# Seven products in place of eight for one more pair of feed-forward groups, with two of four weight-block sums made by adding DMAs

## The chip, the cores and the metric

The kernel runs on one core of a Trainium2 chip. The metric is device time in microseconds (us). The engines are named as in the profile: PE (TensorE, matmul), DVE (VectorE), ACT (ScalarE), POOL (GpSimd) and SP (SyncE, which in this kernel issues all loads).

## The reference

Two stacks of two layers each are applied to one sequence of 256 tokens of width 1024, in float32. Each layer is feed-forward, mixer, feed-forward, with norms between; so there are eight feed-forwards and four mixers. The change concerns the feed-forwards, which all have a hidden width of 2816:

```python
D_MODEL = 1024
SEQ = 256
DEPTH = 2
D_FF = 2816
...
def swiglu(x, w13, w2):
    a, b = jnp.split(x @ w13, 2, axis=-1)
    return (jax.nn.silu(a) * b) @ w2
...
    for l in range(DEPTH):
        x = layer_norm(ALPHA * x + 0.5 * swiglu(x, ffn1_w13[l], ffn1_w2[l]), ln_g[l, 0], ln_b[l, 0])
        m = mixer(x, w_in[l], lower_bounds[l], hg_norm_g[l], sg_ln_g[l], sg_ln_b[l], sg_ws[l],
                  sg_bs[l], w_branch_a[l], w_branch_b[l], w_out[l])
        x = layer_norm(ALPHA * x + m, ln_g[l, 1], ln_b[l, 1])
        x = layer_norm(ALPHA * x + 0.5 * swiglu(x, ffn2_w13[l], ffn2_w2[l]), ln_g[l, 2], ln_b[l, 2])
```

## The kernel before

The 256 tokens are two tiles of 128, i = 0 and 1. All weights stream from HBM as blocks of 128 x 1024 float32 (512 KB), each used once; the host lays them out in the order of use (`_ffn_units`, `_stream`). One such block is a unit. SP loads it (`fetch`) into a stage tile `stg`, or, if it belongs to a pair (below), into a tile `raw` of the pool `whp`. Then `split` makes two parts of it: ACT rounds it to `wh` (line 268), DVE subtracts and gets `wl` (line 274). A product of float32 accuracy is three matmuls with 512 moving columns: x-high with `wh`, x-high with `wl`, x-low with `wh`. Units that are not of a pair are split in two halves of 512 columns (two ACT and two DVE instructions); in mixer 2 POOL subtracts the second half of every third unit between 8 and 28. Units of a pair are split whole.

A feed-forward has 11 groups of 256 hidden columns (4 units each, gate and up part side by side) and 22 units of the output matrix (rows, "r"). The first two groups (`OWN`) are done by each token tile for itself. Then `joint` runs a hand-written list, `FFN`, for both tiles at once: ("g", n) is group n done plainly; ("r", k) is output row block k; ("s", n, ks...) is a pair, `pair`: groups n and n + 1 together, as a 2 x 2 by 2 x 2 block product after Strassen and Winograd. Its four weight blocks are called 11, 12, 21, 22 (half of the contraction, gate or up); seven products p1, p2, q5, p3, p6, p7, q4 take the place of eight, each with two units and 12 matmuls (line 547). Four of the seven need sums of weight blocks. DVE makes these in place in the `raw` tiles (`operand`): for q5 and p6 at line 245, for p7 at 249, for q4 at 253, each twice per pair. The ks are output rows that `on` runs for both tiles in the gaps after the products listed in `GAPS`. After some products ACT copies the PSUM bank to a tile `kp`/`kq` (501), DVE adds to it (504), ACT takes silu, DVE multiplies (511), and two steps later PE transposes the result (286; its high and low parts are then made at 294 and 295). The last six output rows (`LAST`) run tile by tile.

How far `split` runs ahead of the matmuls is set by `lead`: PAIR units within reach of a pair, otherwise LEAD plus up to MORE. Loads run STAGES = 4 units ahead of `split`. PE, DVE and ACT orders come out of a scheduler; SP and POOL run in program order. POOL does the power in each norm (410, 619), some mixer work, and, in four of the feed-forwards, products of gain rows (570, 631, 633).

Of the kernel before, what the change touches and what calls it, by code (L numbers as in the profile page):

```python
# [11 lines left out]
F32 = mybir.dt.float32  # L12
# [3 lines left out]
ALU = mybir.AluOpType  # L16
# [3 lines left out]
P = 128  # L20
# [16 lines left out]
RAMP = 3  # L37
STEP = 1
TAIL = 2
PAIR = 5  # L40
LAGS = dict(ffn=9, mixer1=6, mixer2=6)
STAGES = 4
SLOTS = 31
# [10 lines left out]


OWN = 2
FFN = (("g", 8), ("s", 2, 0, 1, 2, 3), ("g", 9), ("s", 4, 16, 17, 4, 5), ("g", 10), ("s", 6, 6, 7, 18, 19),
       ("r", 8), ("r", 9), ("r", 20), ("r", 21))
LAST = (10, 11, 12, 13, 14, 15)


PRODUCTS = ("p1", "p2", "q5", "p3", "p6", "p7", "q4")
LOADS = dict(p1="11", p2="21", q5="12", p3="22")
BLOCKS = ("11", "21", "12", "22")
GAPS = ("p1", "q5", "p6", "p7")


PRM_BS, PRM_LB, PRM_CW, PRM_CB, PRM_N = 0, 8, 16, 96, 112
# [6 lines left out]
def hs(h):  # L75
    return slice(h * P, (h + 1) * P)


class Core:
# [125 lines left out]
    def lead(self):  # L205
# [3 lines left out]
        left = dict(ffn=len(_ffn_units()), mixer1=56, mixer2=36)[kind] - n  # L209
        if self.product(min(self.pos[0] + PAIR, self.nunit - 1)):  # L210
            return PAIR
        return LEAD + (MORE if n < FIRST else max(0, MORE - left // RAMP))
# [11 lines left out]
    def fetch(self, v):  # L224
        while self.next_dma <= min(v, self.nunit - 1):
            made = self.made[self.next_dma]
            if not self.product(self.next_dma):
                t = self.stages[self.next_dma] = self.stg.tile([P, 1024], F32, tag="stg", name=self.nm("stg"))
                for c in (slice(0, 512), slice(512, 1024)) if self.next_dma == 0 else (slice(0, 1024),):
                    self.nc.sync.dma_start(t[:, c], self.a["ws"][made][:, c])  # L230
            elif made[0] in LOADS:
                t = self.raw[made[:2]] = self.whp.tile([P, 1024], F32, tag="w", name=self.nm("raw"))
                self.nc.sync.dma_start(t, self.block(LOADS[made[0]], *made[1:]))
            self.next_dma += 1

# [3 lines left out]
    def operand(self, p, u, base):  # L239


        raw, add = self.raw, self.nc.vector.tensor_add
        if p in ("q5", "p6"):
            t = raw["p1", u]
            add(t, t, raw["q5" if p == "q5" else "p3", u])  # L245
            return t
        if p == "p7":
            t = raw.pop(("p3", u))
            add(t, t, raw.pop(("q5", u)))  # L249
            return t  # L250
        if p == "q4":
            t = raw.pop(("p1", u))
            add(t, t, raw.pop(("p2", u)))  # L253
            return t
        return raw[p, u]

    def split(self, u):
        while self.next_split <= min(u, self.nunit - 1):
            v = self.next_split
            self.fetch(v)  # L260
            made = self.made[v]
            product = self.product(v)
            w = self.operand(*made) if product else self.stages.pop(v)
            hi = self.whp.tile([P, 1024], F32R, tag="w", name=self.nm("wh"))
            lo = self.whp.tile([P, 1024], F32R, tag="w", name=self.nm("wl"))
            halves = [slice(0, 512), slice(512, 1024)]
            for h, c in enumerate([slice(0, 1024)] if product else halves):
                r = self.nc.scalar.activation(hi[:, c], w[:, c], AF.Copy)  # L268
                if v < 3:
                    self.pin(r)  # L270
                if h and self.pool_share(*self.phase[v]):
                    self.nc.gpsimd.tensor_tensor(lo[:, c], w[:, c], hi[:, c], op=ALU.subtract)
                else:
                    self.nc.vector.tensor_sub(lo[:, c], w[:, c], hi[:, c])  # L274
            self.units[v] = [hi[:, c] for c in halves], [lo[:, c] for c in halves]
            self.next_split += 1
            self.fetch(v + STAGES)

    def pool_share(self, kind, n):
# [177 lines left out]
    def joint(self, J, rs):  # L457

        for what, n, *ks in FFN:
            if what == "s":  # L460
# [28 lines left out]
    def pair(self, J, g, ks):  # L489

        nc = self.nc
        first = dict(p1="p1", p2="p2", q5="q5", p3="q5", p6="p1", p7="p1", q4="p1")
        bank, kept, sg = {}, {}, {}
        rows = dict(zip(GAPS[len(GAPS) - len(ks):], ks))

        def keep(p):
            t = kept[p] = self.slot(name="k" + p)  # L500
            nc.scalar.activation(t, bank[p], AF.Copy)  # L501

        def add(t, other):
            nc.vector.tensor_add(t, t, other)  # L504

        def silu(out, src, i):
            rs = J["rs", i]
            nc.scalar.activation(out, src, AF.Silu, scale=1.0 if rs is None else rs)

        def hidden(i, t, sg):  # L510
            nc.vector.scalar_tensor_tensor(t, t, -0.5 if J["rs", i] is None else -1.0, sg,
                                           op0=ALU.mult, op1=ALU.mult)

            def turn():
                hi, lo = self.to_T(t, "hT")
                for c in range(4):
                    J["h", i, 2 * g + c] = hi[:, hs(c)], lo[:, hs(c)]

            self.later(2, turn)

        def after(p):
            if p in ("p1", "q5", "p6", "p7"):
                keep(p)
            if p == "p2":
                t = sg[0] = kept.pop("p1")
                add(t, bank[p])
                silu(t, t, 0)
            elif p == "p6":
                t = kept.pop("p6")
                add(t, bank["p3"])  # L530
                hidden(0, t, sg.pop(0))
            elif p == "p7":
                add(kept["p7"], kept.pop("q5"))
            elif p == "q4":
                t = self.slot(name="sg")
                silu(t, bank[p], 1)
                hidden(1, kept.pop("p7"), t)

        for p in PRODUCTS:
            bank[p] = self.bank(self.grp, "g") if first[p] == p else bank[first[p]]  # L540
            xh, xl = J["X"][p]
            for u in range(2):
                wh, wl = self.units[self.pos[1]]
                for j in range(2):
                    k = 2 * u + j
                    for q, (x, w) in enumerate(((xh, wh), (xh, wl), (xl, wh))):
                        nc.tensor.matmul(bank[p], x[:, hs(k)], w[j], start=first[p] == p and k + q == 0,  # L547
                                         stop=k == 3 and q == 2, skip_group_check=True)
                for i in range(2):
                    self.pos[i] += 1  # L550
                if u:
                    after(p)
                yield
            if p in rows:
                yield from self.on(J, rows[p])
# [1044 lines left out]
```

## Time and profile before

| what | value |
|---|---|
| median of 3 runs | 2171.57 us (2169.29 to 2174.26) |
| the profiled execution's own time | 2170.61 us |
| its span, first to last instruction | 2168.8 us |
| mean granted clock of TensorE | 0.995 |
| busy: PE, DVE, ACT, POOL | 2116.2, 1879.8, 1352.0, 291.4 us |
| HBM read | 391.63 MB |

The span is what the trace covers; the own time has 1.8 us more around it. Busy time is the time in which an engine has at least one instruction in flight, so a pipelined engine can be busy throughout and yet be slower than it could be.

### The profile page before, as it was taken

To read this page: it belongs to the slowest core of one execution; us is meant where nothing else is said; L and a number is where in the kernel's file an instruction comes from. 1 tells how busy PE (TensorE), PEld (TensorE's weight loads), DVE (VectorE), ACT (ScalarE), POOL (GpSimd) and SP (SyncE) were. 2 spreads that over 40 slices of the span, in tenths; PEclk is the share of its full clock that TensorE was granted. 3 is DMA by queue.
4 is the path that set the end of the run, shared out by engine and by line. 5 is a ranking of instruction groups with operands and counts; after the bars stand their busy time and mean duration, and the time that the engine had idled before them with its cause. 6 is when DMAs were issued, how large, how long until landed. Compare 5 with 4: busy or idle time off the path is not lost.

```text
span 2168.8 us, 28670 instructions
## 1 busy us (share of the span) xinstructions
PE 2116.2 (98%) x9968; PEld 1738.6 (80%) x9968; DVE 1879.8 (87%) x2837; ACT 1352.0 (62%) x2351; POOL 291.4 (13%) x319
## 2 busy tenths in 40 slices
PE   8999999999999999999999999999999999999998
PEld 6877888888788788888778787788778878788887
DVE  7998787899889879698989988689998998877995
ACT  6665755566566575565656665666666666576663
POOL 0000420000000033000100304610200010550000
PEclk9999999999999999999999999999999999999999
DMA  8547455455654655545555553434655546343552
GB/s 301 185 176 244 148 190 193 141 213 201 208 190 175 218 160 180 178 159 197 199 197 203 204 194 122 165 117 148 233 195 186 182 172 219 111 152 127 205 192 97
DMA packets 115296, 394.55 MB, mean 182 GB/s; under 512 B 12880, under 2 KB 15312, under 8 KB 115152
## 3 DMA queue, kind: packets, MB, share of 16 engines
q1 hardware_dynamic: 115152, 392.73, 52.5%
q8 instruction: 78, 1.28, 0.2%
q14 instruction: 66, 0.54, 0.1%
HBM read 391.63 MB, written 1.05 MB: 181 GB/s over the span
## 4 chain that ended last, share of the span: by engine, by line
PE 80%; DVE 10%; issue 3%; ACT 3%; POOL 2%; DMA 2%; SPq 0%; DVEq 0%; POOLq 0%; ACTq 0%
PE g L302 33%; PE big L302 23%; PE g L547 17%; DVE wl L274 5%; PE g L286 4%; ACT wh L268 2%; DMA stg<-in_ws_dram 2%; PE big L1262 1%; PE big L1291 1%; PE big L792 1%; DVE raw L245 1%; DVE kp L504 0%; DVE raw L249 0%; PE big L1209 0%; POOL cu L1135 0%
## 5 line engine op out<-in xcount | busy, mean ns | idle before, releaser
L274 DVE TENSOR_TENSOR wl<-stg,wh 128x512 fp32r<-128x512 f32 x1026 | 691.8, 708 | 129.6 <-ACT wh L268 123.3
L268 ACT ACTIVATE wh<-stg 128x512 fp32r<-128x512 f32 x1040 | 600.8, 623 | 200.8 <-PE g L302 83.8
L302 PE MATMUL g<-wh,xh 128*128 128x512 f32 x1184 | 483.1, 408 | 9.3 <-ACT wh L268 5.9
L302 PE MATMUL g<-wl,xh 128*128 128x512 f32 x1184 | 467.2, 395 | 0.5 <-DVE wl L274 0.5
L302 PE MATMUL g<-wh,xl 128*128 128x512 f32 x1184 | 465.3, 395 | 0.0
L268 ACT ACTIVATE wh<-raw 128x1024 fp32r<-128x1024 f32 x336 | 349.3, 1056 | 178.1 <-DVE raw L253 53.7
L274 DVE TENSOR_TENSOR wl<-raw,wh 128x1024 fp32r<-128x1024 f32 x336 | 410.2, 1236 | 25.1 <-ACT wh L268 23.1
L302 PEld LDWEIGHTS g<-wh,xh 128*128 128x128 f32 x1184 | 225.5, 190 | 58.8 <-ACT wh L268 7.3
L302 PEld LDWEIGHTS g<-wh,xl 128*128 128x128 f32 x1184 | 224.7, 190 | 50.4 <-DVE xl L311 2.0
L302 PEld LDWEIGHTS g<-wl,xh 128*128 128x128 f32 x1184 | 225.7, 191 | 43.4 <-DVE wl L274 1.8
L302 PE MATMUL big<-wh,hT 128*128 128x512 f32 x640 | 183.3, 390 | 0.0
L547 PE MATMUL g<-wh,Xh 128*128 128x512 f32 x384 | 149.7, 390 | 1.1 <-ACT kp L501 1.1
L547 PE MATMUL g<-wl,Xh 128*128 128x512 f32 x384 | 150.7, 393 | 0.0
L547 PE MATMUL g<-wh,Xl 128*128 128x512 f32 x384 | 150.2, 391 | 0.0
L302 PEld LDWEIGHTS big<-wh,hT 128*128 128x128 f32 x640 | 120.1, 188 | 25.3
L410 POOL TENSOR_TENSOR m<-m,nhalf 128x1 f32<-128x1 f32 (+1 forms) x24 | 23.1, 962 | 794.5 <-DVE m L409 794.5
L302 PE MATMUL big<-wh,hTh 128*128 128x512 f32 x384 | 124.8, 392 | 0.0
L302 PE MATMUL big<-wl,hTh 128*128 128x512 f32 x384 | 124.2, 390 | 0.0
L302 PE MATMUL big<-wh,hTl 128*128 128x512 f32 x384 | 124.0, 390 | 0.0
L245 DVE TENSOR_TENSOR raw<-raw,raw 128x1024 f32<-128x1024 f32 x96 | 120.6, 1268 | 0.5
L547 PE MATMUL g<-wh,xh 128*128 128x512 f32 x288 | 114.6, 398 | 1.4 <-ACT kp L501 1.4
L547 PE MATMUL g<-wl,xh 128*128 128x512 f32 x288 | 112.5, 391 | 0.0
(322 smaller groups left out, 3229.2 us busy)
## 6 DMA issues: line engine op xcount, KB each, us to landing
stg<-in_ws_dram SPq DMA_DIRECT2D x519, 512.0 KB, 4.4
raw<-in_ws_dram SPq DMA_DIRECT2D x192, 512.0 KB, 5.0
row<-in_norm_gain_dram SPq DMA_DIRECT2D x24, 256.0 KB, 6.8
row<-in_ln_g_dram SPq DMA_DIRECT2D x12, 256.0 KB, 4.9
row<-in_ln_b_dram SPq DMA_DIRECT2D x12, 256.0 KB, 6.3
xT<-in_xT_dram SPq DMA_DIRECT2D x4, 256.0 KB, 6.1
x<-in_x_dram SPq DMA_DIRECT2D x4, 256.0 KB, 8.7
out_dram<-x SPq DMA_DIRECT2D x4, 256.0 KB, 2.0
```

The lines of the kernel that those rows point to most:

```text
L245: add(t, t, raw["q5" if p == "q5" else "p3", u])
L268: r = self.nc.scalar.activation(hi[:, c], w[:, c], AF.Copy)
L274: self.nc.vector.tensor_sub(lo[:, c], w[:, c], hi[:, c])
L286: self.nc.tensor.transpose(tp[:, hs(j)], src[:, hs(j)], self.ident)
L302: self.nc.tensor.matmul(accs[c], a, b[c], start=start and q == 0, stop=stop and q == 2)
L410: self.nc.gpsimd.tensor_tensor(out, out, self.nhalf[:, 0:n], op=ALU.pow)
L547: nc.tensor.matmul(bank[p], x[:, hs(k)], w[j], start=first[p] == p and k + q == 0, stop=k == 3 and q == 2, skip_group_check=True)
L792: nc.tensor.matmul(ps[:, 64 * h:64 * h + 64].rearrange("p (c m) -> p c m", m=m), Z[:, hs(h)], view(Z[:, hs(h)], m)[:, :, 1, :], start=True ...
L1262: nc.tensor.matmul(ps[:, hh * S + j * P:hh * S + j * P + P], J["aq", i][r, hs(head // 2)], J["ak", j][r, hs(head // 2)], start=True, stop= ...
L1291: nc.tensor.matmul(o[:, 64 * hh:64 * hh + 64], pT[:, hs(2 * hh + j)], J["av", j][:, head * 64:head * 64 + 64], start=j == 0, stop=j == 1)
```

## The change

There are now four pairs and three plain groups per feed-forward (before: three and five). The order of the seven products is p1, q5, p3, p6, p2, p7, q4. DVE still makes the sums for q5 and p6, in the same tiles. The sums for p7 and q4 are made by DMA: as soon as p6's block has been split, POOL issues two DMAs that load a weight block from HBM a second time and add it onto the tile that lies there already (`added`): block 12 onto the tile of p3, block 21 onto that of p1. That is four such DMAs per pair, 128 in all, of 512 KB each. Units outside of pairs are split whole instead of by halves (all but the first eight of the program and those that POOL shares). PAIR goes from 5 to 6. The list of output rows in the gaps and the weights' layout follow.

```diff
-PAIR = 5
+PAIR = 6
...
-FFN = (("g", 8), ("s", 2, 0, 1, 2, 3), ("g", 9), ("s", 4, 16, 17, 4, 5), ("g", 10), ("s", 6, 6, 7, 18, 19),
-       ("r", 8), ("r", 9), ("r", 20), ("r", 21))
-LAST = (10, 11, 12, 13, 14, 15)
-
-
-PRODUCTS = ("p1", "p2", "q5", "p3", "p6", "p7", "q4")
-LOADS = dict(p1="11", p2="21", q5="12", p3="22")
-BLOCKS = ("11", "21", "12", "22")
-GAPS = ("p1", "q5", "p6", "p7")
+FFN = (("g", 10), ("s", 2, 0, 1, 2, 3), ("s", 4, 20, 21, 4, 5), ("s", 6, 6, 7, 8, 9), ("s", 8, 10, 11, 12),
+       ("r", 13))
+LAST = (14, 15, 16, 17, 18, 19)
+
+
+PRODUCTS = ("p1", "q5", "p3", "p6", "p2", "p7", "q4")
+LOADS = dict(p1="11", q5="12", p3="22", p2="21")
+BLOCKS = ("11", "12", "22", "21")
+GAPS = ("q5", "p6", "p2", "p7")
...
         if p in ("q5", "p6"):
-            t = raw["p1", u]
-            add(t, t, raw["q5" if p == "q5" else "p3", u])
+            t = raw["p1", u, base]
+            add(t, t, raw.pop(("q5", u, base)) if p == "q5" else raw["p3", u, base])
             return t
-        if p == "p7":
-            t = raw.pop(("p3", u))
-            add(t, t, raw.pop(("q5", u)))
-            return t
-        if p == "q4":
-            t = raw.pop(("p1", u))
-            add(t, t, raw.pop(("p2", u)))
-            return t
-        return raw[p, u]
+        return raw.pop((dict(p7="p3", q4="p1").get(p, p), u, base)) if p in ("p2", "p7", "q4") else raw[p, u, base]
+
+    def added(self, p, u, base):
+        if p == "p6":
+            for q, b in (("p3", "12"), ("p1", "21")):
+                self.nc.gpsimd.dma_start(self.raw[q, u, base], self.block(b, u, base), accum_op=ALU.add)
...
-            for h, c in enumerate([slice(0, 1024)] if product else halves):
+            for h, c in enumerate([slice(0, 1024)] if product or v >= 8 and not self.pool_share(*self.phase[v]) else halves):
...
             self.next_split += 1
+            if product:
+                self.added(*made)
...
-            if p == "p2":
-                t = sg[0] = kept.pop("p1")
+            if p == "p6":
+                add(kept["p6"], bank["p3"])
+            elif p == "p2":
+                t = kept.pop("p1")
                 add(t, bank[p])
                 silu(t, t, 0)
-            elif p == "p6":
-                t = kept.pop("p6")
-                add(t, bank["p3"])
-                hidden(0, t, sg.pop(0))
+                hidden(0, kept.pop("p6"), t)
```

The first place is DVE's order in the first pair of the second feed-forward. Before, from p3's second block (first row) to p7's first block (last row); L249 and L253 are the sums for p7 and q4, `stg` are gap rows:

```order
L274 TENSOR_TENSOR wl_3963<-raw_3897,wh_3962 128x1024
L249 TENSOR_TENSOR raw_3872<-raw_3872,raw_3739 128x1024
L274 TENSOR_TENSOR wl_3976<-raw_3649,wh_3975 128x1024
L249 TENSOR_TENSOR raw_3897<-raw_3897,raw_3848 128x1024
L504 TENSOR_TENSOR kp_940_3929<-kp_940_3929,g_3955 128x512
L274 TENSOR_TENSOR wl_3988<-raw_3681,wh_3987 128x1024
L274 TENSOR_TENSOR wl_4014<-stg_3953,wh_4013 128x512 x2
L253 TENSOR_TENSOR raw_3649<-raw_3649,raw_3714 128x1024
L274 TENSOR_TENSOR wl_4021<-raw_3872,wh_4020 128x1024
```

In the changed kernel the stretch of the same pair from p6's first block (`raw_3468`, the tile of p1) to p7's first block (`raw_3539`, the tile of p3) reads, with L271 for the subtraction, L245 for the sum for p6, `raw_3711` and `raw_3739` for the two blocks of p2:

```order
L271 TENSOR_TENSOR wl_3734<-raw_3468,wh_3733 128x1024
L245 TENSOR_TENSOR raw_3492<-raw_3492,raw_3559 128x1024
L441 SCALAR_TENSOR_TENSOR sg_3701<-g_3630,sg_3701 128x256
L271 TENSOR_TENSOR wl_3751<-raw_3492,wh_3750 128x1024
L441 SCALAR_TENSOR_TENSOR sg_3704<-g_3631,sg_3704 128x256
L450 TENSOR_TENSOR hT_3723<-g_3720,hT_3723 128x256
L271 TENSOR_TENSOR wl_3774<-stg_3687,wh_3773 128x1024
L271 TENSOR_TENSOR wl_3778<-raw_3711,wh_3777 128x1024
L450 TENSOR_TENSOR hT_3729<-g_3726,hT_3729 128x256
L271 TENSOR_TENSOR wl_3794<-raw_3739,wh_3793 128x1024
L271 TENSOR_TENSOR wl_3812<-stg_3756,wh_3811 128x1024
L271 TENSOR_TENSOR wl_3816<-raw_3539,wh_3815 128x1024
```

The sums for p7 and q4 have left DVE, the gap rows' pairs of half subtractions have become one, and five other blocks stand between the split of p6's first block and that of p7's first block.

The second place is POOL's queue in a feed-forward of the second stack. Before, between the powers of two norms (L410, L619) there are only the products of gain rows:

```order
L619 TENSOR_TENSOR m_10404<-m_10404,nhalf 128x1
L631 TENSOR_TENSOR xg_11244<-x_10267,row_11097 128x512
L633 TENSOR_TENSOR gg_11246<-row_11093,row_11097 128x512
L631 TENSOR_TENSOR xg_11245<-x_10271,row_11099 128x512
L633 TENSOR_TENSOR gg_11247<-row_11095,row_11099 128x512
L631 TENSOR_TENSOR xg_11358<-x_10393,row_11097 128x512
L631 TENSOR_TENSOR xg_11359<-x_10397,row_11099 128x512
L619 TENSOR_TENSOR m_11888<-m_11888,nhalf 128x1
```

In the changed kernel the same products of gain rows (L629, L631) stand behind the adding DMAs of three pairs and ahead of those of the fourth:

```order
L252 DMA raw_10636<-in_ws_dram 128x1024
L252 DMA raw_10554<-in_ws_dram 128x1024
L629 TENSOR_TENSOR xg_10752<-x_9779,row_10588 128x512
L631 TENSOR_TENSOR gg_10754<-row_10584,row_10588 128x512
L629 TENSOR_TENSOR xg_10753<-x_9783,row_10590 128x512
L631 TENSOR_TENSOR gg_10755<-row_10586,row_10590 128x512
L629 TENSOR_TENSOR xg_10839<-x_9899,row_10588 128x512
L629 TENSOR_TENSOR xg_10840<-x_9903,row_10590 128x512
L252 DMA raw_10881<-in_ws_dram 128x1024
L252 DMA raw_10816<-in_ws_dram 128x1024
...
L617 TENSOR_TENSOR m_11337<-m_11337,nhalf 128x1
```

The adding DMAs are new in this queue; each waits there, in order, for the DVE and ACT instructions that still read its tile.

## Rows read from the trace of the kernel before

**Rows 1.** The page, part 1: busy us, share of the span, instructions.

```profile
PE 2116.2 (98%) x9968; PEld 1738.6 (80%) x9968; DVE 1879.8 (87%) x2837; ACT 1352.0 (62%) x2351; POOL 291.4 (13%) x319
```

**Rows 2.** The page, part 4: chain that ended last, share of the span.

```profile
PE 80%; DVE 10%; issue 3%; ACT 3%; POOL 2%; DMA 2%; SPq 0%; DVEq 0%; POOLq 0%; ACTq 0%
```

**Rows 3.** Timeline of PE, six matmuls of a pair: start, duration, what.

```profile
1005.06 0.39 PE L547 MATMUL g<-wh,xh 128*128 128x512 f32 x1
...
1006.20 0.39 PE L547 MATMUL g<-wh,xl 128*128 128x512 f32 x1
1006.43 0.27 PE L286 MATMUL g<-con,sg 128*128 128x128 f32 x1
```

**Rows 4.** Groups of PE: count, busy us, mean ns, idle before.

```profile
L302 PE MATMUL g<-wh,xh 128*128 128x512 f32 x1184 | 483.1, 408 | 9.3 <-ACT wh L268 5.9 <-ACT xh L310 3.1 <-ACT xh L164 0.2
...
L547 PE MATMUL g<-wh,Xh 128*128 128x512 f32 x384 | 149.7, 390 | 1.1 <-ACT kp L501 1.1
```

**Rows 5.** Waits of PE: us in total, times, longest.

```profile
PE g L286 <- DVE x L593: 10.3, 10, 1.4
PE g L286 <- DVE kp L511: 7.3, 6, 1.8
...
PE g L286 <- DVE sg L445: 4.8, 7, 0.9
...
PE g L547 <- ACT kp L501: 2.5, 2, 1.4
```

**Rows 6.** Windows in one feed-forward: PE, PEld, DVE, ACT, POOL busy, clock, DMA share, GB/s.

```profile
1020.00:1040.00 20.00, 19.01 (x86) 15.18 (x84) 20.00 (x22) 12.31 (x19) 7.00 (x4) 1.00 0.53 185
1040.00:1060.00 20.00, 18.72 (x86) 15.21 (x87) 19.95 (x24) 11.35 (x17) 0.00 (x0) 1.00 0.65 236
```

**Rows 7.** Chain in time there: first DVE piece, PE piece that ends it.

```profile
1013.92 0.69 DVE kp L504
...
1041.28 0.63 PE g L286 x4
```

**Rows 8.** Timeline of DVE there: start, duration, what.

```profile
1021.38 1.21 DVE L274 TENSOR_TENSOR wl<-raw,wh 128x1024 fp32r<-128x1024 f32 x1
1022.52 1.21 DVE L249 TENSOR_TENSOR raw<-raw,raw 128x1024 f32<-128x1024 f32 x1
...
1025.92 1.21 DVE L274 TENSOR_TENSOR wl<-raw,wh 128x1024 fp32r<-128x1024 f32 x1
1027.06 1.28 DVE L274 TENSOR_TENSOR wl<-stg,wh 128x512 fp32r<-128x512 f32 x2
1028.26 0.68 DVE L504 TENSOR_TENSOR kp<-kp,g 128x512 f32<-128x512 f32 x1
1028.86 1.21 DVE L274 TENSOR_TENSOR wl<-raw,wh 128x1024 fp32r<-128x1024 f32 x1
```

**Rows 9.** The page, part 3: packets, MB, share of 16 engines.

```profile
q1 hardware_dynamic: 115152, 392.73, 52.5%
```

**Rows 10.** DMA issues: count, KB each, median us to landing.

```profile
stg<-in_ws_dram SPq DMA_DIRECT2D x519, 512.0 KB, 4.4
raw<-in_ws_dram SPq DMA_DIRECT2D x192, 512.0 KB, 5.0
```

**Rows 11.** The busiest window of DMA seen, columns as in rows 6.

```profile
480.00:500.00 20.00, 20.00 (x96) 16.52 (x95) 19.61 (x26) 13.64 (x22) 0.00 (x0) 1.00 0.93 346
```

**Rows 12.** Instructions on raw tiles: duration ns min/median/max.

```profile
L274 DVE TENSOR_TENSOR wl<-raw,wh x336: 1201/1219/2335, 35.3 to 2122.5; 128x1024 fp32r<-128x1024 f32 x168
```

**Rows 13.** Groups of POOL, columns as in rows 4.

```profile
L631 POOL TENSOR_TENSOR xg<-x,row 128x512 f32<-128x512 f32 x20 | 35.2, 1761 | 230.6 <-DMA row<-in_norm_gain_dram 129.0 <-DVE wl L274 63.1 <-PE g L286 28.4
```

More of the change, by code (lines that the diff above doesn't have):

```diff
@@ L231, in fetch @@
             elif made[0] in LOADS:
-                t = self.raw[made[:2]] = self.whp.tile([P, 1024], F32, tag="w", name=self.nm("raw"))
+                t = self.raw[made] = self.whp.tile([P, 1024], F32, tag="w", name=self.nm("raw"))
                 self.nc.sync.dma_start(t, self.block(LOADS[made[0]], *made[1:]))
@@ L495, in pair @@
         first = dict(p1="p1", p2="p2", q5="q5", p3="q5", p6="p1", p7="p1", q4="p1")
-        bank, kept, sg = {}, {}, {}
+        bank, kept = {}, {}
         rows = dict(zip(GAPS[len(GAPS) - len(ks):], ks))
```

## The prediction

> **What bounds the kernel now.** I read the page first. PE is busy for 2116.2 us of 2168.8, DVE for 87%, ACT for 62%, POOL for 13% [rows 1], and the chain that ended last lies on PE for 80% and on DVE for 10% [rows 2]. So PE is the bound, with DVE close behind it. "Busy" needs care: a matmul with 512 columns is listed with 0.39 us, but in the timeline of a pair six of them start within 1.37 us, one every 0.228 us [rows 3]. That pitch is what a removed matmul gives back where nothing else holds PE up.
>
> Next, how much PE loses to waiting. It is idle for 2168.8 - 2116.2 = 52.6 us [rows 1], and the first matmul of a trio stands with 408 ns where an undisturbed one has 390: 1184 x 18 ns = 21 us more of stretched matmuls [rows 4]. Together some 74 us. Among the waits named, 7.3 + 4.8 us are transposes that wait for DVE at the end of a group or pair and 2.5 us are products that wait for ACT's copy of a bank; 10.3 us are transposes behind a norm [rows 5].
>
> Where DVE is the bound shows in the windows of a feed-forward: from 1020 to 1060 us DVE is busy for 39.95 us of 40 and PE for 37.7 [rows 6], and the chain runs from a DVE piece at 1013.92 to a PE piece at 1041.28, through DVE, ACT and issue alone [rows 7]. DVE's own pitch is read there too: a block of 1024 columns takes 1.14 us from start to start (subtraction or sum alike), two halves 1.20 us, a short instruction of 512 columns 0.60 us [rows 8].
>
> **The change part by part.**
>
> *Fewer matmuls.* Two plain groups done for both token tiles are 2 groups x 4 units x 2 tiles x 2 halves x 3 = 96 matmuls; a pair is 7 x 12 = 84. One more pair in each of eight feed-forwards: 96 matmuls fewer, x 0.228 us = **21.9 us**. They stand on PE, which sets the end, so all of it counts as long as PE stays the bound. The transposes stay eight for two groups either way.
>
> *DVE in a pair.* Before: 14 subtractions and 8 sums of 1.14 us, four gap rows of 1.20 us, and seven short instructions (three sums onto kp, two multiplications, two low parts) of 0.60 us: 25.1 + 4.8 + 4.2 = 34.1 us. PE needs 84 x 0.228 + 4 gap rows x 12 x 0.228 + about 1 us for eight transposes = 31 us. DVE is 3 us over in each pair; the plain groups between the pairs (PE 10.9 us; DVE 4 x 1.20 us and short work of 2.4 us at most) let it catch up. After: 14 + 4 + 4 instructions of 1.14 us and 4.2 us = 29.3 us against the same 31. So DVE no longer falls behind in a pair, and four pairs in a row do no harm by themselves. What it falls short of now is small: the spare 1.7 us per pair is also its only reserve.
>
> *Whole blocks.* 1.14 us in place of 1.20 us per unit on DVE saves little. In exchange, what waits in DVE's queue behind a block waits up to 0.54 us longer, and a unit's first half is ready later by as much. Where this could reach PE is the norms: 24 chains, once each, at most 24 x 0.54 = 13 us lost. The first units after a norm are split ahead of it, so I charge a third, 4 us.
>
> *Relief of the waits.* At best all of the named 14.6 us and the 21 us of stretch go: 36 us. At worst none goes and the norms lose 13 us. The 14.6 us are the nearest rows; stretch also has causes that stay (the first trio after a norm, slow clock after an idle stretch). I take 16 us, less the 4 us above: **12 us**.
>
> *The adding DMAs: engines' time.* The trace before has none. From below, one costs what a plain load of 512 KB costs; from above I know no limit in it. Plain loads: 392.73 MB in 52.5% of 2168.8 us [rows 9] is 345 GB/s while the engines work; in the busiest window 346 GB/s at a share of 0.93 [rows 11] is 372. So 0.524 MB takes all 16 engines for 1.41 to 1.52 us, 1.46 in the middle. A pair loads eight blocks and four gap rows, 17.5 us of the 31. That leaves 13.5 us for four adds: 3.4 us each, or 2.3 plain loads. An add reads two things and writes one, so I take two plain loads, 2.9 us: 29.2 us of 31. This fits, with 6% to spare, and is the narrowest place of the change. The Trainium skill (Collectives: The Full Stack, The bandwidth ceiling) says that a reducing transfer runs at half the speed of a copy because it reads two sources, measured at 1.93; by that the four adds would take 11.3 us and the pair 28.8 us. No trace here shows it yet.
>
> *The adding DMAs: when they land.* In DVE's new order five subtractions and one sum of 1.14 us stand between p6's first subtraction, which frees the tiles, and p7's first: 6.8 us and some short work. A plain `raw` load lands 5.0 us after its issue [rows 10]; with one more transfer of 1.46 us, 6.5 us, with two more, 8. So the tile is ready about when it is due. If it is late, ACT's rounding of p7's block waits; queued behind it are the following roundings and the copies kp and kq that the next product's bank needs. PE feels that only after the units that are split ahead are used up: six of them (PAIR) from p6 on, which with two gap rows are 4 x 1.37 + 2 x 2.74 = 11 us. I charge nothing; without that cover each late us would count, 32 times.
>
> *POOL.* If issuing an add holds POOL as long as a product of gain rows, 1.76 us [rows 13], that is 7 us of 31, hidden. In three feed-forwards of the second stack six such products (10.6 us) stand in POOL's queue ahead of the fourth pair's adds, and four products of gain rows in one more; they were due about 20 us before those adds, so they matter only if their rows come late. The powers of the norms come after all adds and wait for none.
>
> *Order, PAIR, SP.* The bank copies have as many products between writer and reader as before, except in the fourth pair, which has no gap after q5; there the scheduler puts p6 before p3. SP issues the same number of loads in nearly the same order. No charge.
>
> Sum, on the profiled execution's own 2170.6 us (1 us under the median): 2170.6 - 21.9 - 12 = 2136.7, **2137 us**.
>
> **The rivals.**
>
> *DMA becomes the bound in the pairs (slower).* For it: 29 of 31 us by my own price. Against: in the windows around it DMA is at 0.53 and 0.65 [rows 6], and loads run ahead. At three plain loads per add (4.4 us) a pair takes 35 us; 4 x 4 us per feed-forward, less some 11 us that the lead gives, 8 x 5 = 40 us: 2177 us. At four, 40.9 us, 8 x 29 = 229 us: 2366 us. It turns from gain to loss at 3.0 plain loads per add. Chance 0.15.
>
> *The relief does not come.* Adds land late and hold up ACT, or POOL's descriptor work holds DVE. For the latter: where POOL worked for 7.00 us [rows 6], DVE's subtraction stood at up to 2335 ns against a median of 1219 [rows 12], 1.1 us more. Four times per pair is 4.5 us: DVE would be at 33.8 us of 31, as before, and only the matmuls' 22 us would be left: 2149 us; with late adds on top up to 2165. The Trainium skill (SBUF, State Buffer, Who interferes with whom) says that DVE with two inputs contends with POOL instructions that read SBUF, not with ones that only write it, and descriptors are written; by that this part would cost nothing. Chance 0.20.
>
> *The relief is nearly complete.* PE's waits on DVE vanish and the norms lose nothing: 2170.6 - 22 - 36 = 2113 us. Chance 0.08.
>
> *The gain is cancelled.* An add at about 2.9 plain loads, or norms at 13 us and late adds: within 4 us of before. Chance 0.05.
>
> **How the numbers follow.** My forecast, 2125 to 2150 us around 2137, has 0.52. A difference of 0.2% (4.3 us) is about what a measurement of this kernel tells from none. Faster: 0.52 + 0.20 + 0.08 = 0.80, less 0.01 for late adds at their worst: 0.79. Same: 0.05 + 0.01 = 0.06. Slower: 0.15. For 8 in 10 the range takes the forecast, the missing relief, most of the full relief and the mild end of the DMA case: 2112 to 2178 us.
>
> **What would show it.** Right: 96 matmuls fewer with the pitch kept; DVE below PE in windows of a pair; fewer transposes (286) waiting for 511 and 445; adding DMAs that land within some 8 us; DMA share of 0.8 to 0.95 in the pairs. Wrong: ACT's roundings of `raw` waiting long for DMA; a DMA share of 1; DVE's 1024-column instructions stretched beside POOL's issues; longer waits of the transposes behind norms.

## The result and the profile after

The changed kernel takes 2310.49 us (median of 4 runs, 2303.42 to 2315.07) against 2170.83 us beside it: a ratio of 1.0642, interval 1.0624 to 1.0660. It is slower by 140 us where 34 us of gain were forecast. The profiled execution took 2315.07 us, with a span of 2313.1 and a granted clock of 0.967 (before 0.995).

The page of the changed kernel; the first line answers to [rows 1], the queues to [rows 9], the matmul group to [rows 4], the issues to [rows 10]:

```profile
PE 2144.2 (93%) x9872; PEld 1754.7 (76%) x9872; DVE 1852.4 (80%) x2315; ACT 1364.6 (59%) x1901; POOL 395.2 (17%) x447
...
q1 hardware_dynamic: 115152, 392.73, 49.2%
q0 software_dynamic: 18432, 67.12, 15.6%
...
L545 PE MATMUL g<-wh,Xh 128*128 128x512 f32 x512 | 210.9, 413 | 0.2 <-ACT kq L500 0.2
...
raw<-in_ws_dram SPq DMA_DIRECT2D x256, 512.0 KB, 5.4
raw<-in_ws_dram POOLq DMA_DIRECT2D x128, 512.0 KB, 9.7
```

The 96 matmuls are gone (9968 to 9872), and yet PE is busy for 28 us longer, since its matmuls are stretched (413 ns for a group that stood with 390). It is idle for 2313.1 - 2144.2 = 168.9 us, where it was 52.6. So the 144.3 us of longer span are 116.3 us more of idle, 49.9 us more of stretch, and 21.9 us less for the matmuls that went. None of the other four engines became the bound over the span: DVE fell from 87% to 80%.

The waits of the changed kernel show where PE stands; the third and the last two answer to [rows 5]:

```profile
DVE wl L271 <- ACT wh L265: 271.5, 223, 5.7
ACT wh L265 <- DMA raw<-in_ws_dram: 134.3, 57, 6.8
PE g L285 <- DVE kp L510: 119.4, 35, 6.0
PE g L301 <- POOL wl L269: 13.7, 2, 6.8
PE g L285 <- DVE x L591: 4.2, 4, 1.9
PE g L285 <- DVE sg L444: 2.0, 1, 2.0
```

One line is nearly the whole loss: PE's transposes of kp wait for DVE's multiplication (7.3 us before, 119.4 now, 35 times in 32 pairs). The line above it has no counterpart before: ACT's roundings of `raw` blocks wait for DMA.

How the two hang together is read from the timeline of one pair. POOL issues four adds; ACT rounds blocks (L265), copies banks (L500), takes silu (L507); DVE subtracts (L271), adds onto kp (L503), multiplies (L510):

```profile
667.54 0.86 POOL L252 DMA_DIRECT2D raw<-in_ws_dram  x1 [34.85 <-ACT kp L500]
670.25 1.76 POOL L252 DMA_DIRECT2D raw<-in_ws_dram  x2 [1.84 <-DVE wl L271]
672.24 0.86 POOL L252 DMA_DIRECT2D raw<-in_ws_dram  x1 [0.23 <-DVE wl L271]
...
681.68 1.06 ACT L265 ACTIVATE wh<-raw 128x1024 fp32r<-128x1024 f32 x1 [6.26 <-DMA raw<-in_ws_dram]
...
682.77 1.23 DVE L271 TENSOR_TENSOR wl<-raw,wh 128x1024 fp32r<-128x1024 f32 x1 [5.15 <-ACT wh L265]
...
684.07 3.89 ACT L265 ACTIVATE wh<-raw 128x1024 fp32r<-128x1024 f32 x4
...
687.92 0.68 DVE L503 TENSOR_TENSOR kp<-kp,g 128x512 f32<-128x512 f32 x1
...
688.64 0.63 ACT L507 ACTIVATE kp<-kp 128x512 f32<-128x512 f32 x1 [0.67 <-DVE kp L503]
...
690.79 0.68 DVE L510 SCALAR_TENSOR_TENSOR kp<-kp,kp 128x512 f32<-128x512 f32 x1
...
691.62 1.09 PE L285 MATMUL g<-con,kp 128*128 128x128 f32 x4 [4.16 <-DVE kp L510]
...
693.36 1.05 PE L301 MATMUL big<-wh,hTh 128*128 128x512 f32 x2
```

The four adds were issued at 667.54, 670.25, 670.86 and 672.24 and landed 5.3, 5.5, 10.7 and 12.7 us later. The third is that of p7's second block: it landed at 681.60, and ACT, idle for 6.26 us, took the block at 681.68. DVE ran dry behind it for 5.15 us. In ACT's order four more roundings of `raw` (q4's two blocks among them) stand ahead of the silu of kp1 (the tile kp that holds p1, and after p2 the sum of both), and on DVE their subtractions stand ahead of the multiplication. So the multiplication starts at 690.79, and PE, whose order has the transposes of that product two matmuls ahead of the end of p7, stands 4.16 us.

Windows of the changed kernel, columns as in [rows 6], over this pair, over its burst of adds and behind the stall:

```profile
655.00:690.00 35.00, 32.46 (x146) 26.51 (x144) 26.07 (x26) 21.78 (x26) 3.49 (x4) 1.00 0.83 241
670.00:685.00 15.00, 15.00 (x68) 12.43 (x67) 9.13 (x9) 8.74 (x10) 2.62 (x3) 1.00 1.00 235
690.00:700.00 10.00, 8.38 (x33) 7.00 (x34) 9.56 (x10) 5.18 (x7) 0.00 (x0) 0.83 0.54 163
```

Over the 35 us DMA is at 0.83, and DVE is busy for 26.1 us. But from the second add's issue to the last one's landing, 670 to 685 us, DMA is at 1.00: the 16 engines are full there. So it is in every pair: from the first issue to the last landing of a burst (17.8 us in the median) the share is 0.98 in the median of 32 pairs, and 0.90 at the least. Loads of weights that SP issues in these stretches land 7.7 us after issue in the median, the others 4.5. Behind the stall the granted clock falls to 0.83: part of that window runs at 1.2 GHz in place of 2.4, and two matmuls take about 0.85 us there (the last row of the timeline: the next begin at 694.21) in place of 0.46. That is the stretch.

### The profile page after: what moved, and what is told of

Read it like the earlier page. It is cut to its first block, busy times and chain, and to the rows that moved or that the text cites. A ratio compares the mean times of both kernels' runs of the same rounds, so it can differ in the third digit from the quotient of the medians.

```text
span 2313.1 us, 27877 instructions
## 1 busy us (share of the span) xinstructions
PE 2144.2 (93%) x9872; PEld 1754.7 (76%) x9872; DVE 1852.4 (80%) x2315; ACT 1364.6 (59%) x1901; POOL 395.2 (17%) x447
## 3 DMA queue, kind: packets, MB, share of 16 engines
q1 hardware_dynamic: 115152, 392.73, 49.2%
q0 software_dynamic: 18432, 67.12, 15.6%
## 5 line engine op out<-in xcount | busy, mean ns | idle before, releaser
L271 DVE TENSOR_TENSOR wl<-stg,wh 128x1024 fp32r<-128x1024 f32 (+1 forms) x464 | 561.9, 1218 | 139.6 <-ACT wh L265 133.1
L271 DVE TENSOR_TENSOR wl<-raw,wh 128x1024 fp32r<-128x1024 f32 x448 | 559.8, 1268 | 140.0 <-ACT wh L265 138.4
L265 ACT ACTIVATE wh<-raw 128x1024 fp32r<-128x1024 f32 x448 | 464.5, 1055 | 247.3 <-DMA raw<-in_ws_dram 134.3
L265 ACT ACTIVATE wh<-stg 128x1024 fp32r<-128x1024 f32 (+1 forms) x478 | 480.9, 1016 | 211.9 <-PE g L301 73.2
L301 PE MATMUL g<-wh,xh 128*128 128x512 f32 x928 | 379.9, 409 | 10.5 <-ACT wh L265 6.7
L301 PE MATMUL g<-wl,xh 128*128 128x512 f32 x928 | 367.3, 396 | 13.7 <-POOL wl L269 13.7
L252 POOL DMA_DIRECT2D raw<-in_ws_dram x128 | 112.6, 945 | 962.6 <-DVE raw L245 269.9
L545 PE MATMUL g<-wh,Xl 128*128 128x512 f32 x512 | 213.7, 419 | 0.0
L545 PE MATMUL g<-wl,Xh 128*128 128x512 f32 x512 | 212.3, 415 | 0.0
L545 PE MATMUL g<-wh,Xh 128*128 128x512 f32 x512 | 210.9, 413 | 0.2 <-ACT kq L500 0.2
L285 PE MATMUL g<-con,kp 128*128 128x128 f32 x256 | 48.4, 321 | 119.5 <-DVE kp L510 119.4
L245 DVE TENSOR_TENSOR raw<-raw,raw 128x1024 f32<-128x1024 f32 x128 | 154.6, 1219 | 0.9 <-DMA raw<-in_ws_dram 0.5
L545 PE MATMUL g<-wl,xh 128*128 128x512 f32 x384 | 150.3, 391 | 0.0
L545 PE MATMUL g<-wh,xh 128*128 128x512 f32 x384 | 150.2, 391 | 0.0
```

Of the source, the lines that this page charges most:

```text
L245: add(t, t, raw.pop(("q5", u, base)) if p == "q5" else raw["p3", u, base])
L252: self.nc.gpsimd.dma_start(self.raw[q, u, base], self.block(b, u, base), accum_op=ALU.add)
L285: self.nc.tensor.transpose(tp[:, hs(j)], src[:, hs(j)], self.ident)
L301: self.nc.tensor.matmul(accs[c], a, b[c], start=start and q == 0, stop=stop and q == 2)
```

## The experiments

Each run is compared with the kernel before on the same chip. The last three columns are of one profiled execution, whose time can differ from the median (most in e12, where it took 2170.2 us). "Idle" is span less PE's busy time, "kp" PE's wait for kp and its count; the fewer matmuls alone would leave 2116.2 - 21.9 = 2094.3 us of busy PE.

| run | median us | ratio, interval | idle | PE busy | kp |
|---|---|---|---|---|---|
| the changed kernel | 2310.5 | 1.0642 (1.0624 to 1.0660) | 168.9 | 2144.2 | 119.4, 35 |
| e1, sums on DVE | 2235.7 | 1.0321 (1.0293 to 1.0349) | 105.5 | 2123.6 | 19.8, 21 |
| e2, plain second load | 2185.7 | 1.0086 (1.0061 to 1.0112) | 79.5 | 2110.0 | 28.2, 16 |
| e3, p7's adds first | 2290.0 | 1.0565 (1.0540 to 1.0589) | 151.2 | 2140.5 | 101.1, 33 |
| e4, before with whole blocks | 2186.3 | 1.0085 (1.0066 to 1.0104) | 63.9 | 2120.6 | 8.1, 7 |
| e5, two adds | 2205.1 | 1.0158 (1.0142 to 1.0174) | 90.7 | 2112.8 | 23.3, 10 |
| e6, transposes later | 2237.9 | 1.0316 (1.0291 to 1.0342) | 115.3 | 2120.4 | 44.1, 32 |
| e7, halves kept | 2305.3 | 1.0629 (1.0604 to 1.0655) | 164.1 | 2138.7 | 123.3, 32 |
| e8, e5 + e6 + e7 | 2194.4 | 1.0098 (1.0075 to 1.0122) | 88.2 | 2104.8 | 28.7, 7 |
| f1, before with two adds | 2178.6 | 1.0044 (1.0031 to 1.0056) | 57.2 | 2119.7 | 21.1, 18 |
| e10, e8, gain rows after the pairs | 2174.8 | 1.0027 (1.0017 to 1.0037) | 70.3 | 2101.1 | 24.9, 9 |
| e11, plain loads, covered | 2157.9 | 0.9947 (0.9931 to 0.9963) | 62.0 | 2097.3 | 16.3, 16 |
| e12, e8, gain rows at the end | 2177.4 | 1.0031 (1.0021 to 1.0041) | 70.9 | 2097.5 | 21.5, 9 |
| e13, before, gain rows late | 2166.3 | 0.9985 (0.9973 to 0.9996) | 47.6 | 2117.0 | none |
| e14, e12 with four adds | 2241.3 | 1.0332 (1.0306 to 1.0357) | 121.9 | 2117.9 | 60.6, 31 |

**e1: all sums back on DVE.**

```diff
...
-        return raw.pop((dict(p7="p3", q4="p1").get(p, p), u, base)) if p in ("p2", "p7", "q4") else raw[p, u, base]
+        if p in ("p7", "q4"):
+            t = raw.pop(("p3" if p == "p7" else "p1", u, base))
+            add(t, t, raw.pop(("q5" if p == "p7" else "p2", u, base)))
+            return t
+        return raw[p, u, base]
...
-        if p == "p6":
-            for q, b in (("p3", "12"), ("p1", "21")):
-                self.nc.gpsimd.dma_start(self.raw[q, u, base], self.block(b, u, base), accum_op=ALU.add)
+        pass
```

> The changed kernel with the sums for p7 and q4 back on DVE, no adding DMAs; four pairs, whole blocks, new order kept. Theory A (the four adds of a pair land one after another, 2.7 us apart, and hold up ACT): PE's 119 us of waiting at the transposes of kp (DVE kp L510) goes to under 25 us, and DVE with 33.8 us per pair against PE's 31 is a little over, so 2145 to 2170 us. Rival B (four pairs in a row, or the new order of products, are what starves PE): about 2300 us, the transposes' wait stays over 90 us.

Measured 2235.7, between the two. The kp wait falls from 119.4 to 19.8 us, so the adds caused most of it; but DVE is busy for 1979.4 us, 89%. Against the kernel before less the matmuls (2169.0 - 21.9 in these runs) it loses 89 us; 32 pairs in which DVE needs 33.8 us (26 blocks of 1.14 us and 4.2 us) and PE 31 would be 90. In the eight stretches of four pairs DVE is busy for 951 of 968 us, PE for 924. That fits four pairs in a row being bound by DVE when it makes all the sums.

**e2: the second load without adding** (the sums of p7 and q4 are left out).

```diff
-                self.nc.gpsimd.dma_start(self.raw[q, u, base], self.block(b, u, base), accum_op=ALU.add)
+                self.nc.gpsimd.dma_start(self.raw[q, u, base], self.block(b, u, base))
```

> The changed kernel with the adding left out of the four DMAs: they load the same blocks onto the same tiles from the same queue, so the sums for p7 and q4 are left out of the result. Theory A: a load costs half an add, 1.4 us in place of 2.8, so the third of the four lands 3 to 4 us earlier and PE's wait at the transposes falls from 119 to 20 to 50 us: 2175 to 2220 us. Theory A2 (it is POOL's issuing and the queue's latency, not the add): the wait stays over 90 us, 2280 to 2310 us.

2185.7: 125 us of the 140 come with the adding, in the same queue, the same order and the same places. The DMA share from the first issue of a burst to its last landing is 0.86 in the median here (0.98 with the adding), and that stretch takes 11.2 us in place of 17.8. What stays is 17 us over the kernel before, although 96 matmuls are gone.

**e3: the adds of p7 ahead of those of q4 in POOL's queue.**

```diff
-            for q, b in (("p3", "12"), ("p1", "21")):
-                self.nc.gpsimd.dma_start(self.raw[q, u, base], self.block(b, u, base), accum_op=ALU.add)
+            for q, b, v in (("p3", "12", u),) if u == 0 else (("p3", "12", 1), ("p1", "21", 0), ("p1", "21", 1)):
+                self.nc.gpsimd.dma_start(self.raw[q, v, base], self.block(b, v, base), accum_op=ALU.add)
```

> The changed kernel with the order of the four adds on POOL changed: both onto p3's tiles (for p7) first, then both onto p1's (for q4). Theory A: the second block of p7 has the second add and not the third to wait for, 2.7 us or more earlier; the wait at the transposes falls by 2.7 us x 32 = 86 us or more, to 20 to 40 us, and with the clock that is lost behind these waits the time is 2160 to 2215 us. Rival B or A2: within 15 us of 2310.

Missed: 2290.0. Its timeline shows why:

```profile
660.18 0.86 POOL L252 DMA_DIRECT2D raw<-in_ws_dram  x1 [1.01 <-DVE wl L271]
...
671.21 2.96 ACT L265 ACTIVATE wh<-raw 128x1024 fp32r<-128x1024 f32 x3 [3.64 <-DMA raw<-in_ws_dram]
...
674.15 0.63 ACT L507 ACTIVATE kp<-kp 128x512 f32<-128x512 f32 x1
...
677.14 0.63 PE L285 MATMUL g<-con,kp 128*128 128x128 f32 x4 [1.74 <-DVE kp L510]
```

p7's blocks come nearly in time (ACT waits 0.17 us for DMA at one of them), and the fourth add, issued at 660.18, lands 11.0 us later, at 671.18. ACT waits for it with one of q4's roundings, which stands ahead of the silu too. So a late add anywhere ahead of the silu in ACT's order gates kp1, the third in the change and the fourth here; my theory had the place wrong, not the chain.

**e4: the kernel before with whole blocks outside the pairs.**

```diff
-            for h, c in enumerate([slice(0, 1024)] if product else halves):
+            for h, c in enumerate([slice(0, 1024)] if product or v >= 8 and not self.pool_share(*self.phase[v]) else halves):
```

> The kernel before with whole blocks in place of halves alone (same condition as in the change). Theory A: no part of the pairs' loss; at most the 13.7 us that PE waits for POOL's wl in mixer 2 comes from here: 2160 to 2188 us. Rival C (longer instructions in DVE's and ACT's queues are what delays the transposes): over 2200 us, with the wait for kp L511 well over 7 us.

Held: 17 us slower. The wait for POOL in the second mixers is there without any adding DMA. In its timeline, the POOL instruction that delays that `wl`:

```profile
1345.34 6.51 POOL L1127 TENSOR_SCALAR qk<-cv,prm 128x256 f32<-128x256 f32 x1 [5.90 <-DVE cv L980]
```

In the kernel before it stood with 1.10 us.

**e5: two adds, those of q4.**

```diff
+        if p == "p7":
+            t = raw.pop(("p3", u, base))
+            add(t, t, raw.pop(("q5", u, base)))
+            return t
...
-            for q, b in (("p3", "12"), ("p1", "21")):
+            for q, b in (("p1", "21"),):
```

> Only q4's sums come by adding DMAs, p7's are DVE's again; whole blocks as in the change. Theory A (the burst of four adds lands late, and ACT's blocked roundings hold back kp1's silu, on which PE's transposes wait): two adds per pair land about 6.5 and 9 us after their issue and stand behind two more blocks in ACT's order, so the transposes' wait for kp falls from 119 us to below 40 us; DVE then has 24 x 1.14 + 4.2 = 31.6 us per pair against PE's 31 and keeps some of the 66 us that all sums on DVE cost: 2190 to 2235 us. Rival B (an adding DMA costs by itself, by its traffic): half of the loss against plain loads, (2310 - 2186) / 2 = 62 us, stays: about 2250 us. Rival C (DVE bounds four pairs in a row): no better than all sums on DVE, 2236 us or more.

Held for A: 2205.1, kp 23.3. Two adds per pair land 5.8 and 7.4 us after issue (medians over 32 pairs; in the changed kernel 6.5, 9.0, 11.0 and 13.0). Half of the adds gone takes away 105 us, where all of the adding cost 125.

**e6: PE takes the transposes of the first tile's kp 22 matmuls later.**

```diff
-            self.later(2, turn)
+            self.later(2 if i else 7, turn)
```

> The change as it is, but the transposes of the first tile's kp stand 22 matmuls (5 us) later in PE's order; all four adds stay, and ACT's and DVE's orders are as before but for the copies of those transposes. Theory A: PE stands at those transposes only because silu and multiply come late, 2 to 6 us each; with 5 us of other matmuls ahead of them the wait for kp falls from 119 us to below 35 us, the clock rises to about 0.985, and the time is 2165 to 2220 us. Rival B (the late roundings starve the next products' blocks as well): PE then waits for wl or wh of p7 and q4 instead, for about the same, 2270 to 2310 us. Rival C (DMA bound): no change in time, 2300 to 2320 us.

2237.9: 73 us back without touching a DMA, but 18 us short of A's range. Its waits of PE:

```profile
PE g L285 <- DVE kp L510: 44.1, 32, 3.6
PE g L545 <- ACT kp L500: 26.0, 15, 3.0
```

Both theories had a part: most of the loss was where PE's order met the late kp, and a rest moved to the products, which now wait for ACT's copies of a bank.

**e7: halves kept outside the pairs** (the edit of e4 undone in the changed kernel).

> The change with blocks outside the pairs split in halves, as in the kernel before. Theory A: the kernel before lost 17 us by whole blocks alone, 13.7 of it PE's wait for POOL's subtraction in the second mixers; that wait goes and the rest stays: 2290 to 2300 us. Rival B (whole blocks cause part of the late kp, since ACT and DVE are held 0.5 us longer per block ahead of silu and multiply): kp's wait falls from 119 to below 95 us and the time to 2270 us or less.

2305.3: 5 us, intervals that overlap. The kp wait stays (123.3), so whole blocks are no part of it; but one POOL wait of 7.6 us is still there, and the 17 us of e4 don't come back here. Neither theory's number held.

**e8: the edits of e5, e6 and e7 together.**

> Three edits together: q4's sums alone by adding DMAs, the transposes of the first tile's kp 22 matmuls later, and halves outside the pairs. Theory A: the wait for kp is nearly gone (below 15 us), POOL's wait in the second mixers is gone, and what remains is DVE's 31.6 us per pair against PE's 31 and the 21.9 us of matmuls: 2145 to 2180 us. Rival B (four pairs in a row on DVE): 2200 to 2225 us.

Missed by 14 us: 2194.4. Four waits for kp of 5.3 to 6.7 us were left, one in each of four feed-forwards with products of gain rows; each ends 30 to 33 us after the first of these products starts. The timeline ahead of the first wait, which ends at 1061.7:

```profile
1030.55 0.86 POOL L256 DMA_DIRECT2D raw<-in_ws_dram  x1 [1.41 <-PE g L549]
...
1031.12 8.25 POOL L572 TENSOR_TENSOR gr<-row,row 128x512 f32<-128x512 f32 x2
...
1042.02 0.60 ACT L504 ACTIVATE kp<-g 128x512 f32<-128x512 f32 x1 [9.01 <-POOL br L572]
...
1042.65 0.69 DVE L507 TENSOR_TENSOR kp<-kp,g 128x512 f32<-128x512 f32 x1 [5.68 <-ACT kp L504]
```

The first of these two products took 7.00 us, the second 1.29. ACT's next copy waited for POOL, and DVE, with no reserve in a pair, for ACT. In the second of the four feed-forwards it was again a POOL product that stood (7.25 us). In the third and fourth it was DVE, with one subtraction of 8.89 and one of 8.87 us beside six POOL products; two subtractions, the long one among them:

```profile
1571.44 10.02 DVE L275 TENSOR_TENSOR wl<-raw,wh 128x1024 fp32r<-128x1024 f32 x2
```

How the delay reaches PE 30 us later was not followed step by step.

**f1: the kernel before, with q4's sums by adding DMAs.**

```diff
-            t = raw.pop(("p1", u))
-            add(t, t, raw.pop(("p2", u)))
-            return t
+            return raw.pop(("p1", u))
...
+            if product and made[0] == "p6":
+                self.nc.gpsimd.dma_start(self.raw["p1", made[1]], self.block("21", *made[1:]), accum_op=ALU.add)
```

> The kernel before, three pairs and two plain groups in its old order, with one edit: q4's two sums come by adding DMAs issued behind p6's split. DVE falls from 34.1 to 31.8 us per pair against PE's 31. Theory A (the loss of the change is the lateness of a burst of four adds, not an add as such): two adds land about 6 and 7.4 us after issue, as in the run with two adds, and are due behind four more blocks; PE's wait for kp stays below 15 us and the time is 2155 to 2175 us, the same or slightly faster. Rival B (an add costs by its traffic, or POOL's products behind it stretch): 2185 to 2200 us.

2178.6, between the two ranges. kp's wait rose from 7.3 to 21.1 us, over the 15 of theory A: two adds don't pay even where DVE gets 2.3 us per pair back.

**e10: e8 with POOL's products of gain rows 28 units later.**

```diff
-                    self.later(72, lambda: self.pre_gains(i, (l, 2), pre))
+                    self.later(100, lambda: self.pre_gains(i, (l, 2), pre))
...
-                ahead(60, (l, 1), (l, 2))
+                ahead(88, (l, 1), (l, 2))
```

> The run with two adds, later transposes and halves, with POOL's products of gain rows 28 units later, behind the four pairs. In that run one product that starts right behind an add's issue under an unbroken train of DVE stood 7.0 us in place of 1.3, ACT's copy of kp waited 9.0 us for it, and PE stood 5 to 7 us once in each of four feed-forwards of the second stack. Theory A: these four stalls go with their half clock: 2194 - 4 x 6 = 2165 to 2180 us. Rival B (the stall comes from DVE, which needs 31.6 us per pair and falls behind by the third pair): it stays, 2188 to 2198 us.

The time is in A's range: 2174.8, 20 us less. A's reason held in part: of the four waits for kp one went and three stayed, with 5.2, 4.6 and 4.6 us. In these three feed-forwards the products still fell into the last pair, as this stretch of its timeline shows (a block of DVE 2.25 us in place of 1.14, a POOL product 1.97 where others stand with 1.3 to 1.7):

```profile
1263.18 3.94 POOL L633 TENSOR_TENSOR xg<-x,row 128x512 f32<-128x512 f32 x2
1263.69 4.51 DVE L275 TENSOR_TENSOR wl<-raw,wh 128x1024 fp32r<-128x1024 f32 x2
```

PE's idle falls by 17.9 us, of which kp has 3.8; a wait of 7.1 us for POOL's `wl` in a mixer is gone too, and nearly all of the 5.4 us in which products waited for DVE's `wl`. Which of these the move brought is not shown.

**e11: what the change is worth if nothing is late** (e2, so the sums of p7 and q4 are left out, with the edits of e6, e7 and e10).

> What is left of the change without its adding: the four DMAs load without adding (the sums of p7 and q4 are left out), transposes of the first tile's kp later, halves outside the pairs, gain rows behind the pairs. Theory A (lateness was the cause; the saved 96 matmuls are worth 21.9 us where nothing is late): kp's wait below 10 us, the clock at 0.99 or above, 2135 to 2165 us. Rival B (four pairs in a row and the new order cost something else): 2175 us or more.

2157.9, in A's range, though kp's wait is 16.3 us. PE is busy for 2097.3 us, 3 us over what the fewer matmuls alone would leave. So the matmuls' 21.9 us are real, and they end in 11 us of gain (0.5%) against the 2168.9 us of before in these runs.

**e12, e13, e14: the products at the very end** (the edit of e10 with 116 in place of 100; in e13 118), in e8, in the kernel before, and in e8 with all four adds.

> Two adds per pair, later transposes, halves, and POOL's products of gain rows 16 units later still (44 later than in the change). In the run before they still fell in the last pair of three feed-forwards, where DVE's blocks took 1.98 to 2.25 us beside them in place of 1.14, and PE stood 4.75 to 5.4 us soon after. Theory A (collision of POOL's products with DVE's blocks): those three stalls go, kp's wait falls from 24.9 to below 14 us, 2155 to 2168 us, under the kernel before by 0.1 to 0.6%. Rival B (the products now come too late for the norm, or the stall is that of the pairs themselves): 2172 us or more.

> The kernel before with the same move of POOL's products and nothing else. Theory A (PE has gaps in a three-pair feed-forward only where the products fall among the pairs, and the kernel before waits little there): 2163 to 2170 us, the same within 0.3%. Rival B (the move is worth the same in any kernel, 10 us or more): 2160 us or less.

> All four adds as in the change, with later transposes, halves and the late products. Theory A (the burst's last adds land 11 to 13 us after issue and hold back ACT whatever else is mended): between the run with later transposes alone (2238) and that less the other mends (40 us), 2195 to 2225 us, so the third and fourth add cost 30 to 60 us. Rival B (the adds don't matter once the rest is covered): within 10 us of the run with two adds.

e12 missed: 2177.4, within 0.2% of e10. In its profiled execution the waits of 5 us for kp are gone (the longest is 3.0), but the time is not, so these waits were not what remained; the norms' low parts now wait instead (7.7 us for `xl`, 1.3 in e10). e13 held: 2166.3, the same within 0.2%, so the 20 us of e10 are no gain of the move as such. e14 was worse than A's range: 2241.3. Two more adds per pair, those of p7, cost 2241.3 - 2177.4 = 64 us with all else covered and with DVE spared p7's sums. It is no faster than e6 (2237.9): the other edits bring nothing while four adds are there. Its waits show the old chain:

```profile
ACT wh L265 <- DMA raw<-in_ws_dram: 103.1, 52, 6.9
...
PE g L285 <- DVE kp L510: 60.6, 31, 5.7
```

## Why the prediction was wrong, point by point

**Where it failed: "The adding DMAs: when they land".** I worked out 6.5 to 8 us for one add, with one or two more transfers at a plain load's 1.46 us, and the first of a burst does land after 6.5 us. But four go out within 5 us, and they land one behind the other: 6.5, 9.0, 11.0 and 13.0 us after each one's issue, and the landings are 2.9, 3.3 and 3.8 us apart (medians of 32 pairs). p7's second block needs the third, q4's second the fourth. The 2.9 us that I had for the engines' time of one add was in the text, and I did not add it up for the burst: four at the measured 2.82 us (below) are 11.3 us, SP's loads come on top, and the engines are full from 670 to 685 us.

**And the cover: "PE feels that only after the units that are split ahead are used up ... 11 us".** PE did not run out of split blocks. It stood at the transposes of kp1, which hang on a silu and a multiplication queued behind the blocked roundings; e6 takes 73 us out of the loss by moving these transposes alone. The step "Order, PAIR, SP" charged nothing and looked at the bank copies alone. In the new order p2 is the fifth product and no longer the second, so the silu of kp1 has moved from behind the second product to behind the fifth, into the stretch in which the roundings wait, and the multiplication hangs on it there. By itself the order costs little of this: e2 has it too, with 28.2 us for kp. I had written that without the cover each late us would count, 32 times: it was 119.4 us, 35 times 3.4.

**Not priced: the clock.** The stalls brought 50 us more of stretch; with kp's wait at 23 us (e5) PE's busy time is 31 us lower than in the changed kernel.

**Right.** The price of an add: 15.6% of 2313.1 us for 128 adds is 2.82 us of all 16 engines, against 49.2% for 392.73 MB, 1.52 us per plain load of 512 KB: 1.86 plain loads, where I took two. The Trainium skill (Collectives: The Full Stack, The bandwidth ceiling) has 1.93 for a reducing transfer; the trace agrees nearly. The matmuls: e11. DVE below PE in pairs: 26.1 us of 35. That an issue on POOL holds DVE: it doesn't; DVE's subtractions of `raw` blocks stand with 1220 ns in the median beside an issue (64 of them) and 1219 without one. The Trainium skill (SBUF — State Buffer, Who interferes with whom) says so of POOL work that only writes, and the trace agrees. The 2335 ns from which the prediction priced an issue stood at 1539.43 us, beside a product of gain rows and not in the window of [rows 6].

**Right over a pair and wrong in the burst: DMA as the bound.** The share over 35 us is 0.83, under the forecast 29.2 of 31, and no price of three plain loads was needed for the loss. But "this fits, with 6% to spare" spread the adds over the pair, and they come in one burst, in which the engines are full; a DMA share of 1 and ACT's long waits for DMA were both among the prediction's signs of being wrong. How much of the lateness would go if SP's loads kept out of the burst was not run.

**Mis-sized.** Whole blocks: 4 us lost in the sum, 17 alone (e4), 13.7 of it by a wait for POOL in the mixers and not by the norms. The relief: +16 us was to come; even with nothing late (e11) idle is 62.0 us where it was 52.6. The products of gain rows counted as hidden on POOL: in the version with two adds moving them gave 20 us (e10). The rival "the relief does not come" had the mechanism, late adds that hold up ACT, and a top of 2165 us; that was 145 us short.

**What stays open.** e10 is 16.9 us over e11, with the products of gain rows in the same place. Two adds per pair, and DVE's two sums for p7, which e11 leaves out, lie between them; they were not told apart. Why the kernel of e7 keeps one of the two POOL waits is not known either. No run with the sums made beats the kernel before by more than 0.2%.

## What to carry to other kernels

Work that is taken off an engine and given to a queue is priced by when the last of a burst lands, not by the time of one or by the engines' share over a longer stretch, which hides a burst that fills them. Then follow, in each engine's own order, what stands behind the instruction that waits: here a late block stopped a silu that had nothing to do with it, and PE, the bound, stood for that one. Where an engine has no slack, ask for each rare helper instruction (a product on POOL) what it does if it falls among the busy ones.

## What the hardware showed that I had not expected

- Four adds that fill the DMA engines land 2.9, 3.3 and 3.8 us apart, up to 13.0 us after issue, where four plain loads in the same queue (e2) landed 4.9, 6.1, 6.5 and 6.6 us after issue.
- Beside an unbroken run of DVE a POOL instruction stood 5.4 to 5.7 us longer: 7.00 in place of 1.29 (`gr`, e8), 6.51 in place of 1.10 (`qk`, e4). The other way round, a subtraction on DVE stood 8.89 us beside six POOL products (e8), and four of the changed kernel stood 5.26 to 5.72 us beside products of gain rows, in place of 1.22. The Trainium skill (SBUF — State Buffer, Who interferes with whom) says that a DVE instruction with two inputs in SBUF contends with a POOL instruction that reads SBUF. The engines and operands fit that here; the delay lasted over several instructions of the other engine. No run tested the cause.
